# Column mean of an 8192 x 8192 array: another cut of the last row group, the early blocks added by VectorE, one pair load for two single loads

## The chip, the core and the metric

The kernel runs on one core of a Trainium2 chip. A core has a matrix engine (TensorE, PE in the profile), VectorE (DVE), ScalarE (ACT), GpSimd (POOL), a queue engine that only issues transfers and waits (SyncE, SP), and 16 DMA engines between HBM and the on-chip memory SBUF. TensorE writes its products into PSUM, from where VectorE or ScalarE copies them out. The metric is the device time of one execution in microseconds, lower being better.

## What is computed

```python
x = np.random.randn(8192, 8192).astype(np.float32)
return np.mean(x, axis=0)
```

The input has 256 MiB (268.4 MB) and is read once; the output has 32 KiB. All of it is float32.

## The kernel before

**Tiles.** The 8192 rows are taken as G = 64 groups of 128 rows, a group being one row per SBUF partition (4 MiB, 32 KB on a partition). The 8192 columns are counted in 16 blocks of F = 512. One tile `bufs` has six slots of 128 x 8192: four take loads in turn, the fifth (`both`) takes the sum of the two groups of a pair, the sixth (`acc`) is the running sum.

**Order of the loads.** All loads go through SyncE's queue in program order (`load`, line 73). Line 110 loads blocks 0 to 2 of group 60 into `head`; line 111 loads groups 0 to 3 in one transfer and 4 to 5 in another; line 112 loads blocks 8 to 11 of group 63 into `ahead`. The loop at line 118 loads groups 6 to 53 in pairs, two rows to a partition. The loop at line 125 loads groups 54 to 59 one at a time. Lines 129 to 133 load what is left of group 60 (blocks 3 to 15) and the whole of group 61; line 135 loads group 62; line 139 loads group 63 in three parts: blocks 0 to 7 (2 MiB), 12 to 13 and 14 to 15 (512 KiB each). A load waits until the add that read its slot is done, so a load that goes into the slot of group g is issued some time ahead of its turn in the stream.

**The adds.** VectorE adds (`add`, line 93; the instruction has line 95). A pair costs it two adds of 8192 columns, pair to `both` and `both` to `acc`; a single group costs one. Of group 60 it adds blocks 3 to 15, of group 61 blocks 5 to 15. An add that waits for a load gets its wait through a no-op on ScalarE or GpSimd (line 98), which waits for the load and for the add ahead. GpSimd adds blocks 13 to 15 of group 62 to `acc` (line 136).

**The products.** What is not added is summed by TensorE: a product with `ones` (all 1/M, 32 columns) sums the 128 partitions of some columns of a row and accumulates in PSUM. Four products go to the four quarters (32 partitions) of a PSUM tile and may run at once. `plan` (line 142) fixes the order: `ahead`, the sums `acc` as they become final, group 61's blocks 0 to 4, `head`, group 62's blocks 0 to 12, and group 63's three parts as they land. Blocks 0 to 11 have three PSUM tiles of 512 columns (`banks`, four blocks each); blocks 12 to 13 and 14 to 15 have tiles of 256 columns each (`ends`, four products of 256 columns for two blocks).

**The end.** ScalarE copies the three banks and `ends[0]` from PSUM (line 183), VectorE copies `ends[1]` into `tail` (line 201). Four stores follow: blocks 8 to 11 and 12 to 13 from ScalarE's queue, blocks 0 to 7 (`s01`, line 206) and then 14 to 15 (line 208) from SyncE's. SyncE waits for all of them. A no-op on VectorE (line 212) waits until `s01` has landed.

Of the kernel before, what the change touches and what calls it, by code (L numbers as in the profile page):

```python
# [8 lines left out]
@with_exitstack  # L9
def kernel(  # L10
    ctx: ExitStack,
    tc: tile.TileContext,
    x: bass.AP,
    out: bass.AP,
):

    nc = tc.nc
    f32 = mybir.dt.float32
    M, N = x.shape  # L40
    P = nc.NUM_PARTITIONS
    F = 512
    W = F // 2
    WHOLE = 12
    G = M // P
    U = 6
    sync = mybir.DependencyInfo(mybir.DependencyClass.Sync, mybir.DependencyReason.DATA)

    sb = ctx.enter_context(tc.tile_pool(name="sb", bufs=1))
    psp = ctx.enter_context(tc.tile_pool(name="psum", bufs=1, space=bass.MemoryType.PSUM))  # L50

    bufs = sb.tile([P, U, N], f32, name="bufs")
    both = bufs[:, U - 2, :]
    acc = bufs[:, U - 1, :]
    ones = sb.tile([P, 32], f32, name="ones")
    ahead = sb.tile([P, 4 * F], f32, name="ahead")
    tail = sb.tile([P, W], f32, name="tail")
    warm = sb.tile([P, 32], f32, name="warm")
    nc.gpsimd.memset(ones[:], 1.0 / M)  # L59
    ready = sb.tile([P, 1], f32, name="ready")  # L60
    tc.keep_in_program_order(
        nc.gpsimd.tensor_add(out=ready[:], in0=ones[:, 0:1], in1=ones[:, 1:2]))  # L62
    banks = [psp.tile([P, F], f32, name=f"bank{b}") for b in range(3)]
    ends = [psp.tile([P, W], f32, name=f"end{e}") for e in range(2)]

    loads = []

    def landed(*inss):

        nop = tc.keep_in_program_order(nc.sync.nop()).ins  # L70
        for o in inss:
            tc.add_manual_dep(nop, o.name, sync, reason="SyncE waits")

    def load(dst, src):
        ins = tc.keep_in_program_order(nc.sync.dma_start(out=dst, in_=src)).ins  # L75
        k = len(loads)
        over = loads[k - 8:k - 6] if k >= 8 and k % 2 == 0 else []
        tc.declare_no_dep(ins, group="loads", keep=over, reason="the reader of the buffer waited")
        for o in over:
            tc.add_manual_dep(ins, o.name, sync, reason="covers the next load too")  # L80
        tc.add_to_no_dep_group("loads", ins)
        loads.append(ins)
        return ins

    def rows(g, n=1):
        return x[g * P:(g + n) * P, :]

    def load_rows(g, u, n):
        return load(bufs[:, u:u + n, :], rows(g, n).rearrange("(p j) c -> p j c", j=n))

    adds, joins = [], {}

    def add(dst, a, b, dmas):

        ins = nc.vector.tensor_add(out=dst, in0=a, in1=b).ins  # L95
        if dmas and adds:
            waiter = nc.scalar if len(adds) % 8 > 1 else nc.gpsimd
            nop = joins[waiter] = tc.keep_in_program_order(waiter.nop()).ins  # L98
            for o in dmas + adds[-1:]:
                tc.add_manual_dep(nop, o.name, sync, reason="the no-op waits")  # L100
            for group in ("loads", "adds"):
                tc.declare_no_dep(ins, group=group, reason="the no-op waited")
            tc.add_manual_dep(ins, nop.name, sync, reason="waits for both at once")
        elif adds:
            tc.declare_no_dep(ins, group="loads", reason="the add ahead waited")
        tc.add_to_no_dep_group("adds", ins)
        adds.append(ins)

    head = sb.tile([P, 3 * F], f32, name="head")
    load(head[:], rows(G - 4)[:, :3 * F])  # L110
    first, second = load_rows(0, 0, 4), load_rows(4, 4, 2)
    load(ahead[:], rows(G - 1)[:, 8 * F:WHOLE * F])
    add(bufs[:, 2:4, :], bufs[:, 2:4, :], bufs[:, 0:2, :], [first])
    add(bufs[:, 4:6, :], bufs[:, 4:6, :], bufs[:, 2:4, :], [second])
    add(acc, acc, both, [])
    tc.keep_in_program_order(nc.scalar.copy(out=warm[:], in_=ones[:]))  # L116
    g = 6
    while g < G - 10:
        u = (g + 2) % 4
        dma = load_rows(g, u, 2)  # L120
        add(both, bufs[:, u, :], bufs[:, u + 1, :], [dma])
        add(acc, acc, both, [])
        g += 2

    while g < G - 4:
        row = bufs[:, (g + 2) % 4, :]
        add(acc, acc, row, [load(row, rows(g))])
        g += 1
    for lo, loaded in [(3, 3), (5, 0)]:
        row = bufs[:, (g + 2) % 4, :]  # L130
        dma = load(row[:, loaded * F:], rows(g)[:, loaded * F:])
        add(acc[:, lo * F:], acc[:, lo * F:], row[:, lo * F:], [dma])
        g += 1
    r61, r62, r63 = [bufs[:, (g + 1 + j) % 4, :] for j in range(3)]
    load(r62, rows(g))
    tc.keep_in_program_order(nc.gpsimd.tensor_add(  # L136
        out=acc[:, 13 * F:], in0=acc[:, 13 * F:], in1=r62[:, 13 * F:]))
    g += 1
    for lo, hi in [(0, 8), (12, 14), (14, 16)]:
        load(r63[:, lo * F:hi * F], rows(g)[:, lo * F:hi * F])  # L140

    plan = [
        (ahead, 8, 12),
        (acc, 3, 5),
        (acc, 0, 3),
        (r61, 0, 5),
        (head, 0, 3),
        (acc, 5, 12),
        (r62, 0, 12),
        (r62, 12, 13),  # L150
        (acc, 12, 14),
        (acc, 14, 16),
        (r63, 0, 8),
        (r63, 12, 14),
        (r63, 14, 16),
    ]
    sums = []
    for row, lo, hi in plan:
        base = 8 * F if row is ahead else 0
        if lo < WHOLE:  # L160
            for i in range(lo, hi):
                cols = row[:, i * F - base:(i + 1) * F - base]
                sums.append((banks[i // 4], i % 4, cols))
        else:
            for c in range(lo * F, hi * F, W):
                e, q = divmod(c // W - 2 * WHOLE, 4)
                sums.append((ends[e], q, row[:, c:c + W]))
    for n, (dst, q, cols) in enumerate(sums):
        tc.keep_in_program_order(nc.tensor.matmul(  # L169
            out=dst[32 * q:32 * q + 32, :],  # L170
            lhsT=ones[:],
            rhs=cols,
            start=all(d is not dst or k != q for d, k, _ in sums[:n]),
            stop=all(d is not dst or k != q for d, k, _ in sums[n + 1:]),
            tile_position=(0, 32 * q),
            skip_group_check=True,
        ))

    res = both[:, :3 * F].rearrange("p (b c) -> p b c", b=3)
    tails = [both[:, 3 * F:3 * F + W], tail[:]]  # L180

    def copy(dst, src):
        tc.keep_in_program_order(nc.scalar.copy(out=dst, in_=src))  # L183

    def store(engine, dst, src, *then):
        ins = tc.keep_in_program_order(engine.dma_start(out=dst, in_=src)).ins
        for o in then:
            tc.add_manual_dep(ins, o.name, sync, reason="follows that load")
        return ins

    def end(e):
        return (out[(WHOLE + 2 * e) * F:(WHOLE + 2 * e + 2) * F].rearrange("(q c) -> q c", q=4),
                tails[e][0:P:32, :])

    copy(res[:, 2, :], banks[2][:])
    s2 = store(nc.scalar, out[8 * F:12 * F].rearrange("(q c) -> q c", q=4), res[0:P:32, 2, :],
               loads[-3])
    for b in range(2):
        copy(res[:, b, :], banks[b][:])
    copy(tails[0], ends[0][:])  # L200
    nc.vector.tensor_copy(out=tails[1], in_=ends[1][:])  # L201
    landed(*loads[-8:-6])
    landed(*loads[-6:-4])
    landed(*loads[-4:-2])
    landed(*joins.values())
    s01 = store(nc.sync, out[:8 * F].rearrange("(b q c) -> q b c", b=2, q=4), res[0:P:32, 0:2, :])
    s3 = store(nc.scalar, *end(0))
    store(nc.sync, *end(1))
    landed(loads[-2], s2)
    landed(loads[-1], adds[-1])  # L210
    landed(s01, s3)
    hold = tc.keep_in_program_order(nc.vector.nop()).ins
    tc.add_manual_dep(hold, s01.name, sync, reason="VectorE ends late")


# [28 lines left out]
```

## Time and profile before

| | |
|---|---|
| median of 4 runs | 628.63 us (628.51 to 629.13) |
| the profiled execution, its own time | 628.51 us |
| span of its trace | 626.6 us |
| HBM read | 268.44 MB, 428 GB/s over the span |
| VectorE busy | 526.0 us (84%), 60 instructions |
| TensorE busy | 17.3 us (3%), 124 matrix records |
| loads' queue (q1) | 5908 packets, 99.2% of 16 engines' time |
| an add of 8192 columns | 8.70 us |

The span reaches from the first to the last thing the profiler saw; the 1.91 us between it and the execution's own time lie around the span. Each product of 512 float32 columns leaves two matrix records. A `PEld` row is the load of TensorE's stationary operand for one record, `SPq` and `ACTq` are the issuing of transfers by SyncE and ScalarE. In the chain of waits each row tells what the end of the program was waiting for at that moment.

### The profile page before, as it was taken

Reading aid. Unit: us, or ns where it says so; the run is one execution under the profiler, and the core shown is the slowest. Engines: PE = TensorE matmul, PEld = TensorE weight load, DVE = VectorE, ACT = ScalarE, POOL = GpSimd, SP = SyncE. Lnnn points to the kernel's source line nnn. Section 1 sums busy time; section 2 is a strip of 40 time slices with the busy share of each in tenths; the row PEclk is TensorE's granted clock in tenths of the full one; section 3 lists DMA queues with packets and bytes.
Section 4 is the critical chain, followed back from the end, with each engine's and each line's share of the span. In section 5 each row is a group of like instructions: output and inputs, shape, how many; then the busy total and the mean of one; then the engine's idle time right before and its main releaser. Section 6 shows DMA issues by size and latency. Waiting matters only on the chain.

```text
span 626.6 us, 475 instructions
## 1 busy us (share of the span) xinstructions
PE 17.3 (3%) x124; PEld 4.7 (1%) x124; DVE 526.0 (84%) x60; ACT 3.5 (1%) x6; POOL 4.0 (1%) x7
## 2 busy tenths in 40 slices
PE   0000100000000000000000000000000000000027
PEld 0000000000000000000000000000000000000002
DVE  0028999999888998888988889888898888999991
ACT  0000000000000000000000000000000000000001
POOL 0000000000000000000000000000000000000002
PEclk9999999999999999999999999999999999999999
DMA  9999999999999999999999999999999999999997
GB/s 385 469 402 412 459 456 414 448 423 418 452 402 469 402 469 402 469 402 469 402 469 402 469 402 469 402 469 402 460 410 435 435 406 431 435 435 435 423 431 305
DMA packets 5926, 268.50 MB, mean 428 GB/s; under 512 B 656, under 2 KB 664, under 8 KB 1060
## 3 DMA queue, kind: packets, MB, share of 16 engines
q1 hardware_dynamic: 5908, 268.46, 99.2%
q8 instruction: 1, 0.02, 0.0%
q10 hardware_dynamic: 16, 0.01, 0.0%
q14 instruction: 1, 0.01, 0.0%
HBM read 268.44 MB, written 0.03 MB: 428 GB/s over the span
## 4 chain that ended last, share of the span: by engine, by line
DMA 56%; DVE 33%; another core or an unknown queue 10%; issue 0%; SPq 0%; PE 0%; ACTq 0%; POOLq 0%; POOL 0%
DMA bufs<-in_x_dram 56%; DVE bufs L95 33%; SPq L75 0%; PE end L169 0%; ACTq L98 0%; DVE tail L201 0%; POOLq L98 0%; POOL ready L62 0%; POOL ones L59 0%; POOLq L228 0%
## 5 line engine op out<-in xcount | busy, mean ns | idle before, releaser
L95 DVE TENSOR_TENSOR bufs<-bufs 128x8192 f32<-128x8192 f32 (+3 forms) x59 | 525.6, 8909 | 87.8 <-DMA bufs<-in_x_dram 43.5
L169 PE MATMUL bank<-bufs,ones 128*32 128x512 f32 x74 | 11.6, 677 | 540.6 <-DVE bufs L95 540.1
L201 DVE COPY tail<-end 128x256 f32<-128x256 f32 x1 | 0.4, 425 | 10.3 <-PE end L169 10.3
L136 POOL TENSOR_TENSOR bufs<-bufs 128x1536 f32<-128x1536 f32 x1 | 3.5, 3462 | 614.5 <-DMA bufs<-in_x_dram 614.5
L169 PEld LDWEIGHTS bank<-bufs,ones 128*32 128x32 f32 x74 | 2.8, 118 | 549.8 <-DVE bufs L95 542.7
L183 ACT COPY bufs<-bank 128x512 f32<-128x512 f32 x3 | 1.8, 585 | 619.1 <-PE bank L169 619.1
L169 PE MATMUL bank<-ahead,ones 128*32 128x512 f32 x8 | 1.9, 1057 | 65.6 <-DMA ahead<-in_x_dram 65.6
L169 PE MATMUL end<-bufs,ones 128*32 128x256 f32 x36 | 3.3, 384 | 0.1
L169 PE MATMUL bank<-head,ones 128*32 128x512 f32 x6 | 1.9, 600 | 0.0
L169 PEld LDWEIGHTS end<-bufs,ones 128*32 128x32 f32 x36 | 1.4, 109 | 2.4 <-DMA bufs<-in_x_dram 0.9
L116 ACT ACT_TABLE_LOAD x1 | 1.3, 1283 | 0.7 <-PEq L228 0.7
L169 PEld LDWEIGHTS bank<-ahead,ones 128*32 128x32 f32 x8 | 0.2, 140 | 65.6 <-issue 65.6
L183 ACT COPY bufs<-end 128x256 f32<-128x256 f32 x1 | 0.4, 378 | 0.0
L169 PEld LDWEIGHTS bank<-head,ones 128*32 128x32 f32 x6 | 0.4, 108 | 0.6 <-issue 0.6
L116 ACT COPY warm<-ones 128x32 f32<-128x32 f32 x1 | 0.2, 217 | 0.0
L62 POOL TENSOR_TENSOR ready<-ones 128x1 f32<-128x1 f32 x1 | 0.2, 193 | 0.1
L59 POOL MEMSET ones<- 128x32 f32 x1 | 0.1, 124 | 0.3 <-POOLq L228 0.3
L228 POOL MEMSET const-bfloat16-1.0<- 128x1 bf16 x1 | 0.1, 101 | 0.0
L228 POOL MEMSET const-uint8-127<- 128x1 uint8 x1 | 0.1, 101 | 0.0
L228 POOL MEMSET const-float32-0.0<- 128x1 f32 x1 | 0.1, 98 | 0.2 <-issue 0.2
L228 POOL MEMSET const-float32-1.0<- 128x1 f32 x1 | 0.1, 98 | 0.0
## 6 DMA issues: line engine op xcount, KB each, us to landing
bufs<-in_x_dram SPq DMA_DIRECT2D x8, 4096.0 KB, 24.1
bufs<-in_x_dram SPq DMA_DIRECT2D x1, 3328.0 KB
bufs<-in_x_dram SPq DMA_DIRECT2D x1, 2048.0 KB, 20.2
ahead<-in_x_dram SPq DMA_DIRECT2D x1, 1024.0 KB
bufs<-in_x_dram SPq DMA_DIRECT2D x2, 512.0 KB, 21.5
head<-in_x_dram SPq DMA_DIRECT2D x1, 768.0 KB
bufs<-in_x_dram SPq DMA_DIRECT2D x26, 29.9
out_dram<-bufs ACTq DMA_DIRECT2D x1, 8.0 KB
```

The lines of the kernel that those rows point to most:

```text
L59: nc.gpsimd.memset(ones[:], 1.0 / M)
L62: nc.gpsimd.tensor_add(out=ready[:], in0=ones[:, 0:1], in1=ones[:, 1:2]))
L95: ins = nc.vector.tensor_add(out=dst, in0=a, in1=b).ins
L116: tc.keep_in_program_order(nc.scalar.copy(out=warm[:], in_=ones[:]))
L136: tc.keep_in_program_order(nc.gpsimd.tensor_add(out=acc[:, 13 * F:], in0=acc[:, 13 * F:], in1=r62[:, 13 * F:]))
L169: tc.keep_in_program_order(nc.tensor.matmul(out=dst[32 * q:32 * q + 32, :], lhsT=ones[:], rhs=cols, start=all(d is not dst or k != q for d ...
L183: tc.keep_in_program_order(nc.scalar.copy(out=dst, in_=src))
L201: nc.vector.tensor_copy(out=tails[1], in_=ends[1][:])
L228: nc = _bacc.Bacc("TRN2", target_bir_lowering=False, num_devices=1)
```

## The change

Every block is still summed once; what differs is who sums it and in which order it is loaded.

- Group 63 after its early blocks is loaded as blocks 0 to 7, 13 to 15 and 8 (2 MiB, 768 KiB, 256 KiB). The last part is summed by four products of 128 columns into a PSUM tile `last`, blocks 13 to 15 by four products of 384 columns into `three`; blocks 0 to 7 and 9 to 12 use the banks.
- The early blocks are now blocks 13 to 15 of group 60 and 9 to 12 of group 63. They lie side by side in one tile `early`, and VectorE adds all seven to `acc` in one add of 3584 columns after the pair that starts at group 20. TensorE's four products of `ahead` and three of `head` are gone.
- Groups 54 and 55 are loaded as a pair, so four single groups are left (56 to 59).
- Of group 60 blocks 0 to 12 are loaded and added; of group 61 all is loaded and blocks 5 to 15 are added, as before.
- The no-op on VectorE that waited for `s01` is gone.

```diff
-    W = F // 2
-    WHOLE = 12
+    W = F // 4
...
-    ahead = sb.tile([P, 4 * F], f32, name="ahead")
+    early = sb.tile([P, 7 * F], f32, name="early")
...
-    ends = [psp.tile([P, W], f32, name=f"end{e}") for e in range(2)]
+    three = psp.tile([P, 3 * W], f32, name="three")
+    last = psp.tile([P, W], f32, name="last")
...
-    head = sb.tile([P, 3 * F], f32, name="head")
-    load(head[:], rows(G - 4)[:, :3 * F])
+    load(early[:, 4 * F:], rows(G - 4)[:, 13 * F:])
     first, second = load_rows(0, 0, 4), load_rows(4, 4, 2)
-    load(ahead[:], rows(G - 1)[:, 8 * F:WHOLE * F])
+    load(early[:, :4 * F], rows(G - 1)[:, 9 * F:13 * F])
...
-    while g < G - 10:
+    while g < G - 8:
         u = (g + 2) % 4
         dma = load_rows(g, u, 2)
         add(both, bufs[:, u, :], bufs[:, u + 1, :], [dma])
         add(acc, acc, both, [])
+        if g == 20:
+            add(acc[:, 9 * F:], acc[:, 9 * F:], early[:], [])
         g += 2
...
-    for lo, loaded in [(3, 3), (5, 0)]:
+    for lo, hi, loaded in [(0, 13, 13), (5, 16, 16)]:
         row = bufs[:, (g + 2) % 4, :]
-        dma = load(row[:, loaded * F:], rows(g)[:, loaded * F:])
-        add(acc[:, lo * F:], acc[:, lo * F:], row[:, lo * F:], [dma])
+        dma = load(row[:, :loaded * F], rows(g)[:, :loaded * F])
+        cols = slice(lo * F, hi * F)
+        add(acc[:, cols], acc[:, cols], row[:, cols], [dma])
         g += 1
...
-    for lo, hi in [(0, 8), (12, 14), (14, 16)]:
+    for lo, hi in [(0, 8), (13, 16), (8, 9)]:
         load(r63[:, lo * F:hi * F], rows(g)[:, lo * F:hi * F])
 
     plan = [
-        (ahead, 8, 12),
-        (acc, 3, 5),
-        (acc, 0, 3),
+        (acc, 2, 5),
+        (acc, 0, 2),
         (r61, 0, 5),
-        (head, 0, 3),
-        (acc, 5, 12),
-        (r62, 0, 12),
-        (r62, 12, 13),
-        (acc, 12, 14),
-        (acc, 14, 16),
+        (acc, 5, 13),
+        (r62, 0, 13),
+        (acc, 13, 16),
         (r63, 0, 8),
-        (r63, 12, 14),
-        (r63, 14, 16),
+        (r63, 13, 16),
+        (r63, 8, 9),
     ]
...
-    copy(tails[0], ends[0][:])
-    nc.vector.tensor_copy(out=tails[1], in_=ends[1][:])
+    copy(res3, three[:])
+    nc.vector.tensor_copy(out=tail[:], in_=last[:])
...
-    s3 = store(nc.scalar, *end(0))
-    store(nc.sync, *end(1))
+    s3 = store(nc.scalar, part(13, 16), res3[0:P:32, :])
+    store(nc.sync, part(8, 9), tail[0:P:32, :])
...
-    hold = tc.keep_in_program_order(nc.vector.nop()).ins
-    tc.add_manual_dep(hold, s01.name, sync, reason="VectorE ends late")
```

## The prediction

> **What bounds the kernel now.** I read the page's slices first. The DMA row stands at 9 from the second microsecond to the last slice while VectorE leaves gaps, so the stream of loads is the bound, whatever the chain's shares by engine say.
>
> ```profile
> span 626.6 us, 475 instructions
> ...
> DMA  9999999999999999999999999999999999999997
> ```
>
> Then the stretches of one pair's length. Their columns are the stretch, its length, busy time of PE, PEld, DVE, ACT and POOL, the granted clock, the DMA share and GB/s.
>
> ```profile
> 491.30:510.65 19.35, 0.00 (x0) 0.00 (x0) 17.38 (x3) 0.00 (x0) 0.00 (x0) 1.00 1.00 434
> 549.40:568.70 19.30, 0.00 (x0) 0.00 (x0) 19.10 (x3) 0.00 (x0) 0.00 (x0) 1.00 1.01 435
> 588.00:607.40 19.40, 0.05 (x4) 0.05 (x6) 19.08 (x3) 0.00 (x0) 0.00 (x0) 1.00 0.99 426
> ```
>
> 434 GB/s for pairs, as much in the singles at 549, 426 with the cut loads. VectorE has 17.4 of 19.35 us to do per pair, so nearly 2 us of slack. Moving 268.44 MB at 434 GB/s takes 618.5 us of the 626.6: what an edit can win is the few microseconds ahead of and behind the stream. So third, the end of the chain of waits (start, length, what):
>
> ```profile
> 600.97 21.99 DMA bufs<-in_x_dram
> 622.96 0.04 issue
> 623.00 0.68 PE end L169 x8
> 623.69 0.02 issue
> 623.71 0.42 DVE tail L201
> ```
>
> The last load has landed at 622.96; four products, VectorE's copy and the last store follow. The order of time there (start, length, engine, line, operation, and in brackets the idle time before) shows what stands beside:
>
> ```profile
> 615.63 3.46 POOL L136 TENSOR_TENSOR bufs<-bufs 128x1536 f32<-128x1536 f32 x1 [614.50 <-DMA bufs<-in_x_dram]
> 620.50 1.92 PE L169 MATMUL bank<-bufs,ones 128*32 128x512 f32 x16 [0.29 <-DMA bufs<-in_x_dram]
> 621.79 0.16 PEld L169 LDWEIGHTS end<-bufs,ones 128*32 128x32 f32 x4 [0.27 <-DMA bufs<-in_x_dram]
> 622.48 0.58 ACT L183 COPY bufs<-bank 128x512 f32<-128x512 f32 x1 [0.27 <-PE bank L169]
> 623.09 0.71 SPq L186 DMA_DIRECT2D out_dram<-bufs  x1
> 623.37 0.51 ACTq L186 DMA_DIRECT2D out_dram<-bufs  x1
> 624.16 0.56 SPq L186 DMA_DIRECT2D out_dram<-tail  x1
> ```
>
> The last store is issued at 624.16 and the span ends 2.44 us later. I sum against this execution, 628.51 us with 1.91 us around its span; the median of the runs is 0.12 us above it.
>
> **The early blocks.** The two early loads keep their places and sizes (768 KB, 1 MB). VectorE gains one add of 3584 columns: 8.70 x 3584/8192 = 3.81 us, at about 237.8 us. It has 1.95 us of slack per pair, so the next pair's add starts some 2 us late and the one after that about on time. What waits for those adds is a slot: after its pair has landed, an add takes 8.7 us to free a slot, and the stream wants it only when the next pair is in, 19.35 us after. That leaves 10.6 us, and 2 are used. Cost nothing; without that cover it would be 3.8 us. Seven products leave TensorE: four at 65 us, which nobody waited for, three at 611.3, beside the stream.
>
> **One pair for two singles.** The stream first. Group 62 lands at 615.61, 85.75 us after the pair of 52 and 53 (529.86), and 8.81 groups lie between: 9.73 us each, against 38.70/4 = 9.675 in the pairs (491.16 to 529.86, two pairs). 0.055 us per group is what a single costs more; two fewer give 0.1 us. Then VectorE. A pair costs it 17.4 us after landing, so it starts its singles later: pair landed at 549.2, done 566.7; four singles at 8.79 (starts 547.43, 556.23, 565.02) 601.9; group 60's 13 blocks (the row says 7.09) 609.1; group 61's 11 blocks (6.02) 615.2. Now this is 613.4. GpSimd's add wants both this and group 62, which lands at 615.6: 0.4 us to spare, so it stays at 615.6 to 619.1. The slots come free 11 us or more ahead of the stream (group 62 goes where 58 was, free at 593, its turn is 605.4). Cost for the stream nothing.
>
> **TensorE behind it.** Full rate is read from the weight loads at 616.04, 616.47, 616.89: four records per 0.427 us, two per product, so four products of 512 columns take 0.854, of 384 0.64, of 128 0.21. After 615.2: `acc` 5 to 12 1.7, to 616.9; group 62's 13 blocks 2.78, to 619.7; three blocks of `acc` (GpSimd done 619.1) 0.64, to 620.3. Group 63's first part lands at 620.4. It fits, by 0.1 to 0.2 us; before there were 0.3.
>
> **The end.** The stream's last 12 blocks take the same time however cut (8 blocks 4.9 us; two of 512 KB 1.32 and 1.21), so I keep the last landing at 622.9. Eight blocks occupy PE to 622.2, the three blocks (landed 622.25) to 622.91, the last one to 623.12. The old last set took 0.68 of which two halves of 0.213 are columns: 0.26 is pipe. So the last block is out at 623.4. VectorE's copy: 425 ns less 128 columns at 8.70/8192 = 1.06 ns is 0.29 (bounds 0.21, half of it, and 0.425, unchanged): 623.7. That would allow the store at 623.72. But SyncE issues `s01` first, from 623.09 for 0.71 us: it is free at 623.80. **That issue is late next**, so the store goes at 623.82, not 624.16: 0.34 us gained. ScalarE copies three blocks (between 585 ns for 512 columns and 378 for 256, so 0.48) from 623.2 to 623.65, its store is issued 623.68 to 624.19, ahead of the last one's 624.38. The no-op on VectorE waited for `s01`, issued 1.07 us ahead of the last store; I value its removal at nothing. No row shows VectorE ending early, so 0.3 us either way stays open, about the length of the shortest steps here.
>
> The last load's rows on a partition are 2 KB, and no row shows such a load at the end. Below: the 512 KB rows scaled, 0.6 us. Above: it takes as long as 512 KB does, 1.21 us, 0.6 more. I take 0.6, the rate being that of the large loads even at 4 KB rows.
>
> [...]
>
> Sum: 626.6 - 0.34 - 0.1 for the stream is about 626.2, plus 1.91: 628.1. I round up for the thin margin of TensorE: **628.2 us**.
>
> **Rivals.**
>
> *TensorE cold, slower.* The granted clock stands at 1.00, but the rows of the products show two speeds (durations least, median, most; first and last start):
>
> ```profile
> L169 PE MATMUL bank<-bufs,ones x8: 1057/1061/1062, 607.4 to 608.2; 128*32 128x512 f32 x8
> L169 PE MATMUL bank<-bufs,ones x14: 592/592/617, 613.5 to 614.8; 128*32 128x512 f32 x14
> ```
>
> Sets of four records start 0.86 us apart from 607.35 to 610.46 and 0.43 after. TensorE needed 3.1 us of work to reach full rate. Now it gets 10 products at 609.1 where it had 13 at 607.35, ends them at 612.8 (or 613.4 if slow throughout) and idles about 2 us until 615.2; in this profile the weight loads' gap ahead of 613.48 is 1.2 us. If it is slow again, `acc` 5 to 12 takes 3.4 instead of 1.7 and everything behind moves by the amount that 620.3 passes 620.45: bank 1 is out 1.5 us later, `s01` and the last store about 1.2 later than now, 629.7. If it also stays slow in half of group 62's products, 1.4 us more, 631. It decides once TensorE is more than 0.15 us late at group 63's first part. For it: the margin and the gap. Against: the gap is shorter than the work that warms it.
>
> [...]
>
> *The last small part is slow.* It lands 0.6 us later, at 623.5; products and copy end at 624.3, the store goes at 624.3: 628.65.
>
> *The stream gains more.* If the 426 of the last singles' stretch against 434 is their cost, 2% of the 19.35 us that become a pair is 0.35 us: 627.75. To be faster by over 0.2% it would have to win 1.26 us, the sum of all idle steps behind the last landing.
>
> *It does nothing.* Three blocks and one are the same bytes behind the same stream; if the last store is held by something else than `s01`, it stays at 628.5.
>
> **How the numbers follow.** Forecast 58% (627.9 to 628.6); cold TensorE 20%, some half of it beyond 629.77; slow last part 8%; more from the stream 9%, of which 4% beyond 627.25; nothing 5%. The range takes in the stream's 627.75 with 0.15 for the copy's and the no-op's bounds, 627.6, and the milder cold case, 629.7. Within 0.2% (1.26 us, about what a measurement of this kernel can tell) lies all but 10% above and 4% below.
>
> **What would show it.** Right: VectorE's add of 3584 columns near 238 us followed by a pair's add without wait, and adds on time by the second pair after; the last single adds ending at 615.2 with GpSimd's add starting on group 62's landing; the last landing at 622.9 within 0.2; `s01` issued at 623.1 and the last store directly behind it. Wrong: products of 1060 ns after 615 us, TensorE still on group 62 after 620.4, a landing of the last part over 0.8 us after the three blocks, or a last store that waits on VectorE.

## The result, and the profile after

| | before | after |
|---|---|---|
| median | 628.59 us (61 runs) | 629.26 us (41 runs) |
| the profiled execution, its own time | 628.51 us | 629.86 us |
| its span | 626.6 us | 628.0 us |
| ratio after/before | | 1.0011 (95%: 1.0007 to 1.0015) |

The changed kernel takes 0.67 us more. That is within the 0.2% that the prediction speaks of and inside its range, but the forecast of 628.2 us had the sign wrong, and the interval excludes a gain. The profiled execution of after lies 0.60 us above its own median: its adds start 0.5 us behind before's as early as 162 us (162.75 against 162.24) and stay there, which the other kernels with the same early blocks don't repeat (q1 162.21). For sizes I therefore use a kernel that differs from after by the no-op alone (q1 below; its profiled execution took 629.22 us).

The page of after: still the stream of loads from end to end, with a longer span.

```profile
span 628.0 us, 453 instructions
...
DMA  9999999999999999999999999999999999999996
```

The stretches of one pair's length (stretch, length, busy PE, PEld, DVE, ACT, POOL, granted clock, DMA share, GB/s):

```profile
472.35:491.70 19.35, 0.00 (x0) 0.00 (x0) 17.39 (x2) 0.00 (x0) 0.00 (x0) 1.00 1.00 431
492.60:511.95 19.35, 0.00 (x0) 0.00 (x0) 17.38 (x2) 0.00 (x0) 0.00 (x0) 1.00 1.00 434
```

One stretch moves 431 GB/s where its neighbour moves 434, with the DMA engines busy in both. The order of time of VectorE shows the same place: after's add of a pair starts 20.25 us behind the one ahead instead of 19.35, because the load behind it lands late.

```profile
472.35 17.42 DVE L95 TENSOR_TENSOR bufs<-bufs 128x8192 f32<-128x8192 f32 x2 [1.92 <-ACTq L98]
492.60 17.42 DVE L95 TENSOR_TENSOR bufs<-bufs 128x8192 f32<-128x8192 f32 x2 [2.83 <-ACTq L98]
511.97 17.42 DVE L95 TENSOR_TENSOR bufs<-bufs 128x8192 f32<-128x8192 f32 x2 [1.95 <-POOLq L98]
```

In the brackets the idle time goes 1.92, 2.83, 1.95: 0.9 us are lost once and never come back. Before has 1.93 at the second of these adds.

How that load is late can be read too. The trace records the end of every load in 16 parts, each with a packet of 4 bytes. The DMA view of after counts them as "under 512 B", first from 490.8 to 491.3 us, then from 491.3 to 492.5:

```profile
DMA packets 30, 0.98 MB, mean 1966 GB/s; under 512 B 15, under 2 KB 15, under 8 KB 15
```

```profile
DMA packets 2, 0.07 MB, mean 55 GB/s; under 512 B 1, under 2 KB 1, under 8 KB 1
```

Fifteen parts are in together, recorded as landed from 491.35 to 491.65; the sixteenth lands at 492.55, and the add has to wait for it. In before all sixteen lie between 490.87 and 491.16. All 14 loads of after from this one on end like this, one part 0.89 to 0.92 us behind the other fifteen, the last load with fifteen by 623.31 and one at 624.21. So one part in sixteen of the stream falls behind once and stays there, while the rest is on time.

The end of after, in order of time:

```profile
617.03 3.46 POOL L138 TENSOR_TENSOR bufs<-bufs 128x1536 f32<-128x1536 f32 x1 [615.90 <-DMA bufs<-in_x_dram]
621.84 2.09 PE L171 MATMUL bank<-bufs,ones 128*32 128x512 f32 x16
623.36 1.21 ACT L185 COPY bufs<-bank 128x512 f32<-128x512 f32 x2 [1.16 <-PE bank L171]
624.25 0.27 PEld L171 LDWEIGHTS last<-bufs,ones 128*32 128x32 f32 x8 [0.38 <-DMA bufs<-in_x_dram]
624.59 0.71 SPq L188 DMA_DIRECT2D out_dram<-bufs  x1
624.85 0.29 DVE L201 COPY tail<-last 128x128 f32<-128x128 f32 x1 [8.27 <-PE last L171]
625.13 0.52 ACTq L188 DMA_DIRECT2D out_dram<-bufs  x1
625.41 0.55 SPq L188 DMA_DIRECT2D out_dram<-tail  x1
```

The first product of group 63 has no idle time in its row, where before it had 0.29 us and a load as its releaser: TensorE was still at work when the load landed, and the 16 records take 2.09 us instead of 1.92. For the last landing I take the weight load (`PEld`) that it releases, 624.25 here and 623.00 before. `s01` is issued 0.34 us after it, not 0.09. The last store is issued 1.16 us after it, as before, though the last product set and VectorE's copy are shorter.

With q1 the sum closes: last landing 623.54 against 623.00 (+0.54), last store 1.18 us after it against 1.16 (+0.02), from that issue to the end of the span 2.58 against 2.48 (+0.10; before's span is 626.645 us to more places). Together 0.66; the medians differ by 0.67. So most of it is a stream that ends later, and the gain forecast for the end is missing.

### The profile page after: what moved, and what is told of

It reads as the page before. It is cut to its first block, busy times and chain, and to the rows that moved or that the text cites. A ratio compares the mean times of both kernels' runs of the same rounds, so it can differ in the third digit from the quotient of the medians.

```text
span 628.0 us, 453 instructions
## 1 busy us (share of the span) xinstructions
PE 13.4 (2%) x114; PEld 4.7 (1%) x114; DVE 529.8 (84%) x61; ACT 3.7 (1%) x6; POOL 4.0 (1%) x7
## 4 chain that ended last, share of the span: by engine, by line
DMA 52%; DVE 36%; another core or an unknown queue 10%; PE 1%; issue 0%; ACTq 0%; POOLq 0%; POOL 0%
DMA bufs<-in_x_dram 52%; DVE bufs L95 36%; PE bank L171 1%; PE three L171 0%; PE last L171 0%; ACTq L98 0%; POOLq L98 0%; DVE tail L201 0%; POOL ready L61 0%; POOL ones L58 0%; POOLq L226 0%
## 5 line engine op out<-in xcount | busy, mean ns | idle before, releaser
L171 PEld LDWEIGHTS bank<-bufs,ones 128*32 128x32 f32 x74 | 3.5, 118 | 617.5 <-issue 615.3
L95 DVE TENSOR_TENSOR bufs<-bufs,early 128x3584 f32<-128x3584 f32 x1 | 3.9, 3891 | 0.0
L171 PE MATMUL three<-bufs,ones 128*32 128x384 f32 x16 | 2.6, 489 | 0.0
L171 PE MATMUL last<-bufs,ones 128*32 128x128 f32 x24 | 2.1, 274 | 0.0
```

The source lines that it names most:

```text
L171: tc.keep_in_program_order(nc.tensor.matmul(out=dst[32 * q:32 * q + 32, :], lhsT=ones[:], rhs=cols, start=all(d is not dst or k != q for d ...
```

## The experiments

Four theories. **A**: the pair makes VectorE end 1.8 us later, TensorE is late at group 63's first part, and `s01` with it. **B**: the stream itself is longer, by the early loads or their add. **C**: without the no-op the end costs more. **D**, formed after the first four runs: the DMA view of the trace has two packets of a kind called "instruction", one of 8 KB on queue 14 and one of 16 KB on queue 8. What they hold the trace doesn't say. D is my guess from the name: if they bring the engines' own programs, a different number of instructions moves their moment, and in the middle of the stream such a packet takes one of the 16 DMA engines from a load, which then ends with its latest part.

Each kernel ran beside before on the same chip (medians of before 628.57 to 628.61); 11 runs each, 7 of p4 and 8 of t3.

| kernel | median us | minus before | ratio (95%) |
|---|---|---|---|
| p1_no_noop | 629.55 | +0.98 | 1.0016 (1.0007 to 1.0024) |
| p2_pair | 628.80 | +0.23 | 1.0005 (0.9996 to 1.0014) |
| p3_early_add | 629.32 | +0.75 | 1.0012 (1.0003 to 1.0021) |
| p4_cut | 629.70 | +1.13 | 1.0025 (1.0014 to 1.0036) |
| q1_after_noop | 629.38 | +0.78 | 1.0013 (1.0005 to 1.0022) |
| q2_after_scalar_tail | 628.79 | +0.19 | 1.0003 (0.9994 to 1.0012) |
| q3_vector_plus1 | 629.34 | +0.74 | 1.0012 (1.0003 to 1.0021) |
| q4_tensor_plus3 | 628.63 | +0.03 | 0.9999 (0.9991 to 1.0008) |
| r1_cut_less_four | 628.41 | -0.16 | 0.9997 (0.9988 to 1.0006) |
| r2_after_singles | 629.27 | +0.70 | 1.0010 (1.0001 to 1.0019) |
| r3_after_scalar_tail_no_noop | 629.30 | +0.73 | 1.0011 (1.0003 to 1.0020) |
| r4_both_mended | 628.58 | +0.01 | 1.0000 (0.9991 to 1.0009) |
| t1_tensor_plus8_front | 630.05 | +1.44 | 1.0021 (1.0012 to 1.0030) |
| t2_tensor_plus2_late | 628.62 | +0.01 | 1.0000 (0.9991 to 1.0009) |
| t3_cut_same_count | 630.35 | +1.74 | 1.0030 (1.0019 to 1.0040) |
| t4_vector_plus1_no_noop | 629.22 | +0.61 | 1.0006 (0.9997 to 1.0015) |

### One part of the change at a time, on before

**The no-op alone.**

```diff
-    hold = tc.keep_in_program_order(nc.vector.nop()).ins
-    tc.add_manual_dep(hold, s01.name, sync, reason="VectorE ends late")
```

> The kernel before without VectorE's closing no-op, nothing else. Theory A (TensorE comes late to group 63's first part, because VectorE ends its adds 1.8 us later and products of unequal width follow each other): 628.6, no change. Theory B (the stream of loads itself is later, through the early loads or their add): no change. Theory C (the no-op's absence costs at the program's end, outside what the chain shows): 629.0 to 629.3, that is most of the 0.67 us that the whole change lost.

Measured +0.98 us (629.55, above C's forecast). SyncE's waits for the last store (engine, line, what it waited for: us in total, times, longest), first p1, then before:

```profile
SPq L237 <- DMA out_dram<-tail: 1.1, 1, 1.1
```

```profile
SPq L239 <- DMA out_dram<-tail: 0.2, 1, 0.2
```

The wait grows by 0.9 us. The packet of 8 KB starts at 625.55 in p1, 1.2 us after the last store's issue (624.35); in before it starts at 626.25, 2.1 us after it and behind the store's landing (625.80). In p1 it meets the last store: three of the store's four packets start from 625.53 to 625.57, the fourth at 626.02, as the 8 KB packet (0.475 us long) ends, and three parts of the store have landed by 625.95, the fourth at 626.90. So with the no-op, which keeps VectorE from ending, this packet came 0.9 us later behind the store's issue.

**The pair alone.**

```diff
-    while g < G - 10:
+    while g < G - 8:
```

> The kernel before with groups 54 and 55 loaded as a pair, nothing else. Theory A: VectorE's last add ends near 615.2 instead of 613.4, TensorE's margin ahead of group 63's first part shrinks from 0.3 us to nothing; 628.6 to 628.9. Theory B: 628.5, the stream 0.1 us shorter. Theory C: no change.

Measured +0.23 us, an interval that includes none. The trace shows A's steps: the products of group 63 follow those ahead of them without a gap (three of their 16 records start at 620.49, the other 13 from 620.91, where before all of them follow a wait for the load), `s01` is issued 0.54 us after the last landing (623.47 after 622.93) instead of 0.09, the last store 1.36 instead of 1.16.

```profile
620.91 1.88 PE L169 MATMUL bank<-bufs,ones 128*32 128x512 f32 x13
...
623.47 0.71 SPq L186 DMA_DIRECT2D out_dram<-bufs  x1
...
624.29 0.56 SPq L186 DMA_DIRECT2D out_dram<-tail  x1
```

**The early blocks alone**, in two adds, their products taken out of `plan`.

```diff
+        if g == 20:
+            add(acc[:, :3 * F], acc[:, :3 * F], head[:], [])
+            add(acc[:, 8 * F:WHOLE * F], acc[:, 8 * F:WHOLE * F], ahead[:], [])
...
-        (ahead, 8, 12),
...
-        (head, 0, 3),
```

> The kernel before with its two early loads (blocks 0 to 2 of group 60, 8 to 11 of group 63) added by VectorE in two adds after the pair of group 20, and their seven products gone; loads unchanged. Theory A: 628.6, or 0.1 less because TensorE has less to do. Theory B in the form that VectorE's add disturbs the stream: 629.0 to 629.3, with landings 0.4 us later from 240 us on. Theory C: no change.

Measured +0.75 us. The adds themselves are absorbed (at 278.33 VectorE waits 1.60 us for a load again), but at 472.68 a pair's add starts 0.8 us late, and everything stays late. There are two instructions more on VectorE here, one more in after; here the jump is one pair earlier than in after. This led to D: the packet of 8 KB is at 466.35 here, at 476.59 in after, at 626.25 in before.

**The cut alone**, 8, 3 and 1 blocks, the blocks being 0 to 7, 13 to 15 and 12.

```diff
-    for lo, hi in [(0, 8), (12, 14), (14, 16)]:
+    for lo, hi in [(0, 8), (13, 16), (12, 13)]:
...
+        (acc, 12, 13),
...
-        (acc, 12, 14),
-        (acc, 14, 16),
+        (acc, 13, 16),
         (r63, 0, 8),
-        (r63, 12, 14),
-        (r63, 14, 16),
+        (r63, 13, 16),
+        (r63, 12, 13),
```

> The kernel before with the last group cut as 8, 3 and 1 blocks (blocks 0 to 7, 13 to 15, 12), the last in four products of 128 columns; early blocks, pair loop and no-op as before. Theory A: the store order keeps s01 as what is late, 628.2 to 628.5 if TensorE is on time, since VectorE ends at 613.4 here. A rival (the shorter last store's 512-byte rows cost what the shorter products save): 628.6. Theory C: 628.3.

Measured +1.13 us, which none of the theories has. Group 62 lands as before (GpSimd's add of it starts at 615.61, before at 615.63), group 63's first part is late: its products start at 621.85 instead of 620.50, and TensorE waits 1.87 us for it where before it waited 0.29. Again it is one part of the load: fifteen have landed by 620.35, the sixteenth at 621.71 (before: all by 620.36).

```profile
621.85 1.92 PE L171 MATMUL bank<-bufs,ones 128*32 128x512 f32 x16 [1.87 <-DMA bufs<-in_x_dram]
```

The DMA view from 618 to 621 us (queue, kind: packets, MB, share of 16 engines) has the other packet in this kernel; in before it starts at 622.21, behind this landing.

```profile
q1 hardware_dynamic: 146, 1.15, 91.8%
q8 instruction: 1, 0.02, 2.2%
```

Three parts alone cost 0.75 to 1.13 us, four sum to +3.09, and together they cost 0.67. B, as a matter of bytes and adds, doesn't explain that; a thing that has one place or another does.

### Is it the number of instructions?

**One empty instruction on VectorE**, added to before ahead of everything; it sets one column of a tile that nobody reads.

```diff
+    idle = sb.tile([P, 1], f32, name="idle")
+    tc.keep_in_program_order(nc.vector.memset(idle[:], 0.0))
```

> The kernel before with one more VectorE instruction that does nothing useful: a memset of one column into a tile of its own, ahead of the first load's add. Theory D: 629.2 to 629.5, with a jump of 0.7 to 0.9 us in the landings near 470 to 490 us, though nothing that computes has changed. Theories A and B: 628.6, no change.

Measured +0.74 us: as much as the whole change. The order of time of VectorE in this kernel shows after's jump at after's place:

```profile
471.92 17.42 DVE L98 TENSOR_TENSOR bufs<-bufs 128x8192 f32<-128x8192 f32 x2 [1.94 <-ACTq L101]
492.13 17.42 DVE L98 TENSOR_TENSOR bufs<-bufs 128x8192 f32<-128x8192 f32 x2 [2.79 <-ACTq L101]
```

and the DMA view from 470 to 485 us has the packet, as in after (before has only the loads' row there):

```profile
q1 hardware_dynamic: 112, 6.29, 97.2%
q14 instruction: 1, 0.01, 0.1%
```

The instruction writes 128 numbers and touches no load. One part of the load that ends here is late as in after: fifteen by 491.21, one at 492.07. This is the main evidence for D. The place is fixed as well: in all six kernels whose page counts 61 or 62 VectorE instructions (after, p3, q1, q3, r2, t4) the packet starts when 45 of them have started, so p3 with its second extra add has it one add sooner. In the twelve with 60 it comes only after VectorE's last one.

**After with the no-op put back.**

```diff
+    hold = tc.keep_in_program_order(nc.vector.nop()).ins
+    tc.add_manual_dep(hold, s01.name, sync, reason="VectorE ends late")
```

> The changed kernel with VectorE's closing no-op back. Theory D (an 8 KB transfer of VectorE's own program takes one DMA engine away from a load or a store: in the changed kernel its program is one instruction longer and the transfer falls at 476 us into the loads; where the program is short it falls at the end, where the no-op keeps it behind the last store): no change from the changed kernel, 629.1 to 629.4, since no such transfer is left for the end. Theory C (the no-op alone carries the loss): 628.2 to 628.4.

Measured 629.38, no change from after's 629.26, and the jump is there (adds at 471.82 and 491.91). C is not what costs in after: with the packet in mid-stream, none falls beside the last store.

**After with one instruction fewer on VectorE**: the no-op is back, and ScalarE copies the last block.

```diff
-    nc.vector.tensor_copy(out=tail[:], in_=last[:])
+    copy(tail[:], last[:])
...
+    hold = tc.keep_in_program_order(nc.vector.nop()).ins
+    tc.add_manual_dep(hold, s01.name, sync, reason="VectorE ends late")
```

> The changed kernel with the no-op and with the last copy (128 columns) on ScalarE, so that VectorE's program has as many instructions as in the kernel before. Theory D: no transfer of a program at 476 us, the loads 0.7 to 0.9 us earlier, 628.2 to 628.6. Theory A (TensorE late through the pair and the mixed widths): 629.2 or a little more, since all that stays and ScalarE has one more copy to do at the end.

Measured 628.79: 0.59 us less than q1, and 0.2 above D's forecast. The adds start at 472.02 and 491.38 (19.36 apart), the packet is at 626.51. Together, q3 puts the loss on and q2 takes it off, by one instruction.

**The empty instruction without the no-op**, to see whether the two costs add.

```diff
+    idle = sb.tile([P, 1], f32, name="idle")
+    tc.keep_in_program_order(nc.vector.memset(idle[:], 0.0))
...
-    hold = tc.keep_in_program_order(nc.vector.nop()).ins
-    tc.add_manual_dep(hold, s01.name, sync, reason="VectorE ends late")
```

> The kernel before with the idle VectorE memset and without the no-op: two edits that cost 0.74 and 0.98 us one at a time. Theory D (one transfer of 8 KB, which is either among the loads or at the end): 629.3, like the memset alone, with the transfer at 476 us and none beside the last store. If they are separate costs: 630.3.

Measured +0.61, where p1 and q3 alone cost 0.98 and 0.74. The packet is at 475.88 and none lies beside the last store. One transfer, two possible places: that is why the parts don't add.

**After with ScalarE's copy and without the no-op.**

```diff
-    nc.vector.tensor_copy(out=tail[:], in_=last[:])
+    copy(tail[:], last[:])
```

> The changed kernel with the last copy on ScalarE and without the no-op, so that VectorE's program is as short as before and ends early. Theory D: its 8 KB transfer falls beside the last store, whose completion comes 0.8 to 1.0 us later; 629.4 to 629.8. If the no-op matters only with VectorE's late copy: 628.8.

The loss came (+0.73; 629.30, just under the forecast), the place did not. VectorE's last instruction is now its last add, which ends at 615.3, and the packet falls at 619.76, among the loads ahead of group 63's first part (products at 621.39 instead of 620.50), not beside the last store. So in both kernels with 60 VectorE instructions and no no-op the packet came behind the last of them: 4.4 us after its end here, 1.2 in p1.

### The packet of 16 KB

**Three idle products ahead of the first**, into a PSUM tile of their own.

```diff
+    spare = psp.tile([P, 32], f32, name="spare")
+    for q in range(3):
+        tc.keep_in_program_order(nc.tensor.matmul(
+            out=spare[32 * q:32 * q + 32, :], lhsT=ones[:], rhs=ones[:],
+            start=True, stop=True, tile_position=(0, 32 * q), skip_group_check=True))
```

> The kernel before with three more TensorE products of 32 columns, of the ones into a PSUM tile that nobody reads, ahead of the first product. Theory D (extended to TensorE: a 16 KB transfer of its program, at 622.2 in the kernel before and at 619.6 in the run of the cut alone): the transfer comes ahead of group 63's first part, which lands about 1 us later; 629.5 to 629.8. Theory A: no change, 628.6.

Measured +0.03; the packet stays at 622.53. Against D for TensorE, or three are too few.

**Eight of them** (the loop over `range(8)`).

> The kernel before with eight idle TensorE products of 32 columns ahead of the first one (three of them moved nothing). If the moment of the 16 KB transfer is set by the number of TensorE instructions ahead of group 63's first part, with a threshold that three did not reach, it comes at 619.6 and the time is 629.5 to 629.8. If products at the very front do not count, 628.6.

Measured +1.44 us (630.05, above the forecast). The packet has moved to 619.77, and TensorE waits for group 63's first part as in p4:

```profile
622.06 1.92 PE L175 MATMUL bank<-bufs,ones 128*32 128x512 f32 x16 [1.68 <-DMA bufs<-in_x_dram]
```

```profile
q1 hardware_dynamic: 178, 1.13, 90.9%
q8 instruction: 1, 0.02, 2.2%
```

The second fence is the DMA view from 618 to 621 us. Fifteen parts of group 63's first part land by 620.55, one at 621.93. Eight products of 32 columns at the start of the program delayed a load at its end by over 1 us (1.38): D holds for TensorE too.

**p4 with four products fewer**: the sum leaves out `ahead`, blocks 8 to 11 of group 63.

```diff
-        (ahead, 8, 12),
```

> The cut alone (8, 3 and 1 blocks on the kernel before), with the four early products of the blocks 8 to 11 of group 63 left out, so that these blocks miss one group. Nothing at the end of the program differs from the run of the cut alone; TensorE's program is four products shorter. Theory D for TensorE by place in the program: the 16 KB transfer goes back from 619.6 to 622 us or later, and group 63's first part lands at 620.5; 628.2 to 628.5. Rival (the transfer comes at a place counted from the end, or belongs to another engine): 629.7 as with the cut alone.

Measured -0.16 against before, 1.29 us less than p4; the packet is back at 622.35, and TensorE waits 0.50 us for group 63:

```profile
620.65 1.92 PE L170 MATMUL bank<-bufs,ones 128*32 128x512 f32 x16 [0.50 <-DMA bufs<-in_x_dram]
```

**Two idle products directly ahead of group 63's**, the number that p4 adds.

```diff
+        if n == len(sums) - 16:
+            for j in range(2):
+                tc.keep_in_program_order(nc.tensor.matmul(
...
```

> The kernel before with two idle TensorE products of 32 columns directly ahead of those of group 63's first part, as many more as the cut has there (48 for 46). By place in the program: the 16 KB transfer at 619.6 to 620.4, group 63's first part about 1 us later, 629.5 to 629.8. If two small products there change nothing either, 628.6, and what moves the transfer in the run of the cut stays open.

Measured +0.01, a miss for D; the packet doesn't move (622.22). Two more products in p4 move it, two here don't, and three in q4 don't. So TensorE's instructions decide (t1, r1), but not the number of products alone.

**p4 with 62 products**, two blocks moved from TensorE's sum of group 61 to VectorE's.

```diff
-    for lo, loaded in [(3, 3), (5, 0)]:
+    for lo, loaded in [(3, 3), (3, 0)]:
...
-        (acc, 3, 5),
         (acc, 0, 3),
-        (r61, 0, 5),
+        (r61, 0, 3),
...
-        (acc, 5, 12),
+        (acc, 3, 12),
```

> The cut 8, 3 and 1 on the kernel before, complete, but with 62 TensorE products as before (46 ahead of group 63) instead of 64: VectorE adds blocks 3 to 15 of group 61 instead of 5 to 15, 1.1 us more for it. Theory D by TensorE's count: 628.2 to 628.5, no transfer ahead of group 63's first part. Rival (the cut itself moves the transfer): 629.7.

The packet stayed at 622.03 and no load is late, as D has it, yet the kernel took +1.74 us. Something else struck: TensorE gets 12 records, all slow, then idles 5.11 us for VectorE's longer add and is slow behind it too (the profiled execution took 631.07 us).

```profile
614.67 3.64 PE L170 MATMUL bank<-bufs,ones 128*32 128x512 f32 x16 [5.11 <-DVE bufs L96]
```

```profile
L170 PE MATMUL bank<-bufs,ones x41: 592/924/1062, 614.7 to 621.6; 128*32 128x512 f32 x41
```

The second line (durations least, median, most, then first and last start) has a median of 924 ns against 592 in before from 613.5 on. This is the prediction's cold TensorE, in another kernel than the one it was forecast for. It also spoils the test of the count: TensorE is late here, and the packet comes with 36 of its 124 weight loads still to start. Where it has moved 32 (p4) and 34 (t1) are left, where it has not 11 to 16. So by its place in the program it moved here too, with no more products than before, and the rival of the cut itself is not ruled out.

### The pair in after, and the version with all of it mended

**After with before's singles.**

```diff
-    while g < G - 8:
+    while g < G - 10:
```

> The changed kernel with groups 54 and 55 as single loads again (no pair); all else as changed. Theory D plus A as the smaller part: the 8 KB transfer at 476 us stays, TensorE comes on time, the last store is issued 0.2 to 0.4 us earlier after the last landing; 628.9 to 629.1. Without A: 629.3 to 629.4, the stream 0.1 us longer.

A miss: 629.27, the same as after. The trace has TensorE waiting 0.50 us for group 63 again and `s01` 0.18 us after the last landing (623.70 after 623.52), so the lateness of A is gone, but the time doesn't show it.

**After with singles, ScalarE's copy and the no-op**: neither D nor A.

```diff
-    while g < G - 8:
+    while g < G - 10:
...
-    nc.vector.tensor_copy(out=tail[:], in_=last[:])
+    copy(tail[:], last[:])
...
+    hold = tc.keep_in_program_order(nc.vector.nop()).ins
+    tc.add_manual_dep(hold, s01.name, sync, reason="VectorE ends late")
```

> The changed kernel with the last copy on ScalarE, the no-op, and groups 54 and 55 as single loads: neither transfer of a program among the loads, TensorE on time, the small last part. Theories D and A together: 628.2 to 628.5, less than the kernel before by 0.1 to 0.4 us. If something else of the change costs (the add of the early blocks, the 2 KB rows): 628.8 or more.

628.58, a tie with before and less than the gain expected. The end of it in order of time, and SyncE's closing wait:

```profile
623.06 0.18 PEld L171 LDWEIGHTS last<-bufs,ones 128*32 128x32 f32 x8 [0.47 <-DMA bufs<-in_x_dram]
623.23 0.70 SPq L188 DMA_DIRECT2D out_dram<-bufs  x1
623.87 0.52 ACTq L188 DMA_DIRECT2D out_dram<-bufs  x1
624.05 0.55 SPq L188 DMA_DIRECT2D out_dram<-tail  x1
```

```profile
SPq L70 <- DMA out_dram<-bufs: 0.9, 1, 0.9
```

The last store is issued 0.99 us after the last landing, 0.17 sooner than before. SyncE's closing wait is for stores from `bufs`, 0.9 us, and no wait for `tail` shows (before: 0.5 and 0.2). Yet the store from `tail` still lands last, and no sooner: its first packet starts 1.33 us after its issue (625.38), in before 1.20 (625.36), and its last part lands at 625.80 in both. ScalarE's store of the three blocks lies closer ahead of it here, issued at 623.87 instead of 623.37; whether that holds it back wasn't tested. The gain is given back between issue and landing.

## Why the prediction was wrong

**The early add "costs nothing": right in its work, wrong in its instruction.** This is the step that failed. The add of 3584 columns took 3.89 us (3.81 forecast), the next pair's adds and those of the pair after it followed without a wait, and the third pair's waited for its load again:

```profile
238.26 3.89 DVE L95 TENSOR_TENSOR bufs<-bufs,early 128x3584 f32<-128x3584 f32 x1
242.25 34.94 DVE L95 TENSOR_TENSOR bufs<-bufs 128x8192 f32<-128x8192 f32 x4
278.86 17.42 DVE L95 TENSOR_TENSOR bufs<-bufs 128x8192 f32<-128x8192 f32 x2 [1.67 <-POOLq L98]
```

But VectorE has one instruction more (61 in the page, 60 before), and the "instruction" packet of 8 KB moves from behind the last store (626.25) to 476.59 us, where it makes one part of a load, and of all loads behind it, 0.7 to 0.9 us late. The prediction counted the add's microseconds only, and put its price at nothing: in q1 the stream ends 0.54 us later instead of 0.1 sooner. That is the larger part of the miss; the end of the program, 0.12 us longer instead of 0.34 shorter, is the rest. The page of before showed that packet in its own row by queue, at a share of 0.0%; I passed over it.

Among the loads, which take 97.2% of the DMA engines' time there in q3 and 90.9% in t1, such a packet came with a cost of 0.74 us (q3, 8 KB) and of 1.44 (t1, 16 KB).

**The no-op "valued at nothing, 0.3 us either way open": the result in after fits, the bound was too narrow.** In before its removal costs 0.98 us (p1), three times the bound. In after it costs nothing (q1), because the same packet has gone elsewhere (476.59).

**The end, 0.34 us gained: mis-sized.** The parts were right: VectorE's copy 0.29 us as forecast, ScalarE's 0.48 as forecast, the last part 0.63 us behind the three blocks (0.6). In r4 the store is 0.17 us sooner after the last landing. In after it is no sooner, since `s01`, which the prediction named as "late next", was itself late, and the last store follows the start of its issue by 0.82 us (after and r4), not by 0.73. Nor did an earlier issue bring an earlier landing (r4). The time from its issue to the end, taken as 2.44 us (2.48 to more places), became 2.6.

**TensorE "fits, by 0.1 to 0.2 us": wrong.** VectorE's last add ended at 616.59, 1.39 us after the forecast 615.2, as late as after's stream is (1.38 us at the last pair that both have: 531.30 against 529.92). From there to 622.21, where the chain of waits has group 63's products, went 5.58 us of TensorE's work instead of the planned 5.12; products of unequal width lie interleaved there. That made `s01` 0.25 us later after the last landing than before. What it costs in time: p2 and the step from q2 to r4 say some 0.2 us, with intervals that include nothing; r2 says nothing.

**The stream, 0.1 us for the pair: too small to tell.** With the pair alone (p2) the last landing is 0.07 us earlier than before's; q2, with the pair and without the packet among its loads, has 623.02 against 623.00. The working took group 62's landing from GpSimd's start, 615.61; its last part landed at 615.47, which makes a single's extra cost 0.04 us, not 0.055.

**The rivals.** Cold TensorE didn't happen: after the gap the products of 512 columns ran at full rate (median 592 ns from 616.6 on). The gap in the weight loads was 1.66 us here. That a gap makes TensorE slow again was the rival's assumption, and no run shows it: behind p4's 1.87 us of idle time the 16 records took 1.92 us as in before, and ahead of the gap of 5.11 us in t3 the products were slow already (984 to 1061 ns). The slow last part didn't happen. A last store held by something else than `s01` did in r4, between its issue and its landing. That the time lies in the range is no support for the steps: the room above was made for another cause.

**What stays open.** What moves the 16 KB packet among TensorE's instructions: it moved in p4 with two products more than before and, by its place in the program, in t3 with none; in q4 and t2, with three and two idle ones, it didn't. What the waits and other instructions that the page doesn't count weigh in this wasn't tried. Nor is it settled why one VectorE instruction more brings the 8 KB at the 45th, and why in before the 8 KB come only at the end (626.25). That the two packets belong to VectorE and TensorE is read from what moves them; the trace names no owner, and that they bring program text is not shown.

## What to carry to other kernels

In this kernel, whose stream of loads keeps the DMA engines busy (share 1.00 in the stretches of after), an instruction had a price beside its duration: an empty one on VectorE moved the 8 KB "instruction" packet into the stream, and the time rose by 0.74 us (q3). Look for the "instruction" rows by window in the DMA view, before and after an edit, and if one lands among the loads, try one instruction less on that engine. When the parts of a change, measured alone, don't sum to the whole, look for one thing that they all move. And at the end of a program, time the last store to its landing, not to its issue.

## What the runs showed of the hardware

- The 8 KB packet takes 0.32 us in mid-stream, and in after a packet of 64 KB beside it took 3.08 us instead of 2.42; yet the stream loses 0.7 to 0.9 us, because one of a load's 16 parts lands that much behind the others and the load ends with it (after: fifteen by 491.65, one at 492.55). The 16 KB packet takes 1.07 us ahead of group 63's first part, and one part of that load lands 1.4 us behind the others (p4, t1).
- The delay was not made up over 130 us of stream: the late part is 0.90 us behind at 492.55 in after and still 0.90 us behind at 624.21, in q1 0.74 us at 491.85 and 0.73 at 623.50.
- Where VectorE ran out of instructions early, the time rose: by 0.98 us in p1, where the 8 KB packet came 1.2 us after the last store's issue, and by 0.73 us in r3, where it came among the last loads (619.76).
- In after the last load, 256 KB with rows of 2 KB, landed 0.63 us after the one ahead of it; at the 434 GB/s of the large loads it would be 0.60.
